# Attention in a two-layer decoder trunk: score products in two row halves, fp32 value products in two column halves a step later

## The chip, the core and the metric

The kernel runs on one core of one Trainium2 chip. The metric is the device time of one execution in microseconds (us); lower is better. TensorE is the matrix engine, VectorE and ScalarE do elementwise work, GpSimd (POOL) does elementwise work in SBUF, and SyncE (SP) issues the loads. The profile calls them PE (PEld for its weight loads), DVE, ACT, POOL and SP.

## The reference

The input x is 512 tokens by 1024 features, fp32. The model has two layers: an HGRN2 mixer with a conv FFN, then sliding-window attention with a conv FFN, and a final norm. What the change touches is the attention:

```python
def swa_sink_attention(x, k, v, w_q, sinks, w_o):
    q = (x @ w_q).reshape(b_, nb, WINDOW, ATT_KV_HEADS, ATT_GROUP, ATT_HEAD_DIM)
    ...
    scores = jnp.einsum('bnqkgd,bnskd->bnkgqs', q, kb) * ATT_HEAD_DIM ** -0.5
    scores = scores - slopes[:, :, None, None] * dist
    scores = jnp.where(valid[None, :, None, None], scores, -jnp.inf)
    m = jnp.maximum(jnp.max(scores, axis=-1, keepdims=True), sink)
    e = jnp.exp(scores - m)
    probs = e / (jnp.sum(e, axis=-1, keepdims=True) + jnp.exp(sink - m))
    out = jnp.einsum('bnkgqs,bnskd->bnqkgd', probs, vb)
    return out.reshape(b_, s_, ATT_Q_HEADS * ATT_HEAD_DIM) @ w_o
```

There are 16 query heads of 64 features and 2 key/value heads; head j uses key/value head 0 for j below 8 and 1 above. The window is 128, so each block of 128 queries sees its own 128 keys and the 128 before (the first block only its own).

## The kernel before, in words

Activations lie with features on the 128 partitions and the 512 tokens along the free dimension. Large products are done in the type fp32r with each operand split into a high and a low part: `three` (L110 to L113) issues high x high, high x low and low x high into one PSUM bank. `weights` (L94) loads a piece of 128x1024 by SP, copies it to its high part on ScalarE (L104) and subtracts for the low part on VectorE (L105). Plain fp32 products (the transposes, the norm's spread at L186, the HGRN2 products at L323 and L384) are issued without a split, and the profile shows each of the latter as two instructions.

The attention works in 8 steps j. A step handles heads j and j+8 together: the projection `queries(j)` gives one 128x512 bank with the 64 features of head j in the upper half of the partitions and those of head j+8 in the lower. It is a generator, so that its 24 products can be spread between other work: each `step(gen)` issues three of them, and the last also the evacuation (L670) and the split (L674, L675). Before the change the split writes, for each head, a tile whose own half is the high part of the query and whose other half is the low part; the keys' high and low parts stand in both halves (L642 to L645). So two products over all 128 contraction rows (L693) give all four partial products of a head: 8 products for the four blocks of queries. The values are split too, with zeros in the other head's columns (L630, L655, L656), so that all 24 value products of a step (L737) add into one bank `po` of 128 rows.

`softmax` (L696) adds the bias and takes the row maxima on VectorE (L701), exponentiates with a running sum on ScalarE (L708) and scales on POOL (L713). `turn` transposes the probabilities on TensorE (L721), copies them to a high part on ScalarE (L724) and subtracts for the low part on VectorE (L725).

`attend` writes out the order of a step: it interleaves the projection of step j+2, the scores and softmax of step j+1, and the transposes and value products of step j; the value bank is evacuated at its end (L771, L772). `early` fills the last two steps with products of the output projection. The order in which the code names instructions is their priority; a compiler pass orders each engine's queue by it and by readiness and inserts the semaphores. Tiles come from pools: `mm` and `bk` have two PSUM banks each, the score tiles `ax` two pairs of banks, weights three and raw weights four buffers.

Of the kernel before, what the change touches and what calls it, by code (L numbers as in the profile page):

```python
# [50 lines left out]
def trunk(ctx: ExitStack, tc: tile.TileContext, xT, vec, w_qf, w_ig, w_ho, w_kv, w_q, w_o,  # L51
# [19 lines left out]
    def slot(dt=F32):  # L71
        return act.tile([P, S], dt, tag="a", name=nm("a"))
# [4 lines left out]
    def mm_bank():  # L77
        return psm.tile([P, S], F32, tag="mm", name=nm("mm"))
# [16 lines left out]
    def weights(src, n, parts=1, beside=None):  # L95
        raw = wraw.tile([P, 1024], F32, tag="raw", name=nm("raw"))
        hi = wsp.tile([P, 1024], F32R, tag="whi", name=nm("whi"))
        lo = wsp.tile([P, 1024], F32R, tag="wlo", name=nm("wlo"))
        for i in range(parts):
            c = slice(i * n // parts, (i + 1) * n // parts)  # L100
            nc.sync.dma_start(raw[:, c], src[:, c])
            if beside:
                beside[0](i)
            A.copy(hi[:, c], raw[:, c])  # L104
            V.tensor_tensor(lo[:, c], raw[:, c], hi[:, c].bitcast(F32), op=ALU.subtract)  # L105
            if beside:
                beside[1](i)
        return hi, lo
# [27 lines left out]
    class Norm:  # L136
        def __init__(self, gains):
            self.gains = gains
            self.xs = [[None] * KT for _ in gains]
            self.acc = None  # L140
# [328 lines left out]
            flush()  # L469

    class Out:
        def __init__(self, w, piece, m0, banks):
            self.w, self.piece, self.m0, self.banks = w, piece, m0, banks

        def step(self, k, x):
            n = len(self.banks)
            kk = k % (KT // n)
            if kk == 0:
                self.hi, self.lo = weights(self.w[self.piece + k * n // KT], 1024)
            for i, ps in enumerate(self.banks):  # L480
                ws = slice((kk * n + i) * P, (kk * n + i + 1) * P)
                three(ps, self.hi[:, ws], self.lo[:, ws], *x, k == 0, k == KT - 1)
# [142 lines left out]


    halves = [slice(0, HD), slice(HD, P)]
    heads = lambda ap, g: ap.rearrange("p (t d) -> p t d", t=NT)[:, :, g * HD:(g + 1) * HD]
    k_hi, k_lo, v_hi, v_lo = ([slot(F32R) for _ in range(2)] for _ in range(4))
    for x in v_hi + v_lo:  # L630
        G.memset(x.bitcast(F32), 0.0)
    pk = any_bank()
    project(pk, w_kv[0], na.xs[0])
    na.stats()
# [1 line left out]
    project(pv, w_kv[1], na.xs[0], after={3: na.spread})  # L636
    kf = work("fr")
    V.tensor_tensor(kf, pk, na.bc, op=ALU.mult)
    for g in range(2):
        src = kf[halves[g]]  # L640
        own, other = halves[g], halves[1 - g]
        A.copy(k_hi[g][own], src)  # L642
        A.copy(k_hi[g][other], src)
        for dst in (own, other):
            V.tensor_tensor(k_lo[g][dst], src, k_hi[g][own].bitcast(F32), op=ALU.subtract)  # L645
    vf = work("fr")
    V.tensor_tensor(vf, pv, na.bc, op=ALU.mult)

    def token_values():
        pt = any_bank()  # L650
        for t in range(NT):
            ts = slice(t * P, (t + 1) * P)
            PE.transpose(pt[:, ts], vf[:, ts], ident)
        for g in range(2):
            A.copy(heads(v_hi[g], g), heads(pt, g))  # L655
            V.tensor_tensor(heads(v_lo[g], g), heads(pt, g), heads(v_hi[g], g).bitcast(F32),  # L656
                            op=ALU.subtract)

    spans = [(n, P if n == 0 else 2 * P) for n in range(NT)]

    def queries(j, qs):
        pq = mm_bank()
        hi, lo = weights(w_q[j], 1024)
        for k in range(KT):
            ks = slice(k * P, (k + 1) * P)
            three(pq, hi[:, ks], lo[:, ks], *na.xs[1][k], k == 0, k == KT - 1)
            if k < KT - 1:
                yield
        qf = work("qr")
        V.scalar_tensor_tensor(qf, pq, HD ** -0.5, na.bc, op0=ALU.mult, op1=ALU.mult)  # L670
        qs += [work("sg", dt=F32R), work("state", dt=F32R)]
        for g in range(2):
            own, other = halves[g], halves[1 - g]
            A.copy(qs[g][own], qf[own])  # L674
            V.tensor_tensor(qs[g][other], qf[own], qs[g][own].bitcast(F32), op=ALU.subtract)  # L675
        yield

    class Rows:
        def __init__(self, j, g, qs):
            self.hd, self.g, self.qs = j + 8 * g, g, qs  # L680
# [5 lines left out]
        def scores(self):  # L686
# [3 lines left out]
            for n, w in spans:  # L690
                keys = slice((n + 1) * P - w, (n + 1) * P)
                for i, k in enumerate((k_hi[self.g], k_lo[self.g])):
                    PE.matmul(self.sc[:, n, 0:w], self.qs[self.g][:, n * P:(n + 1) * P],  # L693
                              k[:, keys], start=i == 0, stop=i == 1)

        def softmax(self):  # L696
            mx, den, es = (small.tile([P, NT], F32, tag=t, name=nm(t))
# [17 lines left out]
        def turn(self, i):  # L715
            pt = bk_bank()
            width = (4 - i) * P
            for u in range(4 - i):
                n = 2 * i + (u + 1) // 2
                src = self.e[n // 2][:, n % 2, P:] if u % 2 == 0 else self.e[n // 2][:, n % 2, 0:P]  # L720
                PE.transpose(pt[:, u * P:(u + 1) * P], src, ident)  # L721
            eh = work("st" if i == 0 else "kst", dt=F32R)
            el = work("mva" if i == 0 else "fr", dt=F32R)
            A.copy(eh[:, 0:width], pt[:, 0:width])  # L724
            V.tensor_tensor(el[:, 0:width], pt[:, 0:width], eh[:, 0:width].bitcast(F32),  # L725
                            op=ALU.subtract)
            return eh, el

        def values(self, po, i, eh, el):
            vh, vl = v_hi[self.g], v_lo[self.g]  # L730
            for kb in range(2):
                b = 2 * i + kb
                w = P if b == NT - 1 else 2 * P
                src = slice(kb * 2 * P, kb * 2 * P + w)
                ws = slice(b * P, (b + 1) * P)
                for n3, (v, x) in enumerate(((vh, eh), (vh, el), (vl, eh))):
                    PE.matmul(po[:, b * P:b * P + w], v[:, ws], x[:, src],  # L737
                              start=self.g == 0 and b == 0 and n3 == 0,
                              stop=self.g == 1 and b == NT - 1 and n3 == 2,
                              skip_group_check=True)  # L740

    def step(gen, n=1):
        for _ in range(n):
            next(gen, None)

    def attend(rows, nxt, gen):
        a, b = rows
        step(gen, 2)
        for r in nxt[:1]:
            r.scores()  # L750
        po = mm_bank()
        step(gen)
        for r in nxt[:1]:
            r.softmax()
        a0 = a.turn(0)
        for r in nxt[1:]:
            r.scores()
        step(gen, 2)
        a1 = a.turn(1)
        b0 = b.turn(0)  # L760
        a.values(po, 0, *a0)
        for r in nxt[1:]:
            r.softmax()
        step(gen, 2)
        b1 = b.turn(1)
        step(gen)
        a.values(po, 1, *a1)
        b.values(po, 0, *b0)
        b.values(po, 1, *b1)
# [7 lines left out]
    rows = [Rows(0, g, qs[0]) for g in range(2)]  # L777
    step(queries(0, qs[0]), KT)
    gen = queries(1, qs[1])
    step(gen, 4)  # L780
    token_values()
    rows[0].scores()
    step(gen, 4)
    rows[1].scores()
    for r in rows:
        r.softmax()
    outs = []

    def early(j):
        if j == KT - 2:  # L790
            outs.append(Out(w_o, 6, 6, [mm_bank()]))
            for k in range(KT - 2):
                outs[0].step(k, mixed[k])
                yield
        else:
            outs.append(Out(w_o, 4, 4, aux_two()))
            for k in range(KT - 1):
                outs[1].step(k, mixed[k])
# [93 lines left out]
```

## Time and profile before

| | us |
|---|---|
| median of 3 runs | 1203.5 |
| lowest, highest | 1201.35, 1206.54 |
| the profiled execution | 1203.45 |
| its span | 1200.1 |
| PE busy | 1185.0 (99%) |
| DVE busy | 691.1 (58%) |
| ACT busy | 461.7 (38%) |
| POOL busy | 172.0 (14%) |

The span runs from the first to the last instruction that the profile records, and 3.35 us of the execution lie around it. Busy times of PE come from modelled ends of pipelined products, so two that follow each other overlap in the list; the difference of their starts is what one costs in a stream. A row of the timeline with xN is N instructions merged, with the time from the first start to the last end.

### The profile page before, as it was taken

What the parts mean: (1) busy time and instruction counts of PE and PEld (TensorE: products, weight loads), DVE (VectorE), ACT (ScalarE), POOL (GpSimd) and SP (SyncE); (2) the same over time, 40 slices, a digit from 0 to 9 for tenths busy, and PEclk for the clock granted to TensorE, in tenths of its full rate; (3) what the DMA queues carried; (4) which work ended last, traced back from release to release, by engine and by line L of the source; (5) the groups of instructions that cost most, each with busy time, mean ns of one, the idle gap of its engine ahead of it and who ended that gap; (6) DMA issues with size and microseconds to landing.
All of it is one profiled execution on the core that took longest, in us unless ns stands there. A gap on an engine that the chain in (4) does not pass through costs nothing.

```text
span 1200.1 us, 17055 instructions
## 1 busy us (share of the span) xinstructions
PE 1185.0 (99%) x6732; PEld 982.4 (82%) x6732; DVE 691.1 (58%) x1260; ACT 461.7 (38%) x858; POOL 172.0 (14%) x239
## 2 busy tenths in 40 slices
PE   9999999999999999999999999999999999999997
PEld 7888888878888888888888788887888888888887
DVE  6667676665555533555555688646555335555434
ACT  6444444443333222332244577634332222233223
POOL 0011111122111000110112244203111001011001
PEclk9999999999999999999999999999999999999999
DMA  7222222213222233322233211032322343232212
GB/s 244 89 73 80 78 72 71 72 53 106 88 105 77 73 97 123 98 95 84 73 97 121 69 51 43 30 95 84 102 88 66 88 132 101 88 100 94 88 53 71
DMA packets 35087, 105.36 MB, mean 88 GB/s; under 512 B 4032, under 2 KB 7232, under 8 KB 35008
## 3 DMA queue, kind: packets, MB, share of 16 engines
q1 hardware_dynamic: 33920, 103.24, 27.2%
q8 instruction: 52, 0.85, 0.3%
q10 hardware_dynamic: 1088, 1.05, 0.2%
q14 instruction: 27, 0.22, 0.1%
HBM read 102.18 MB, written 2.10 MB: 87 GB/s over the span
## 4 chain that ended last, share of the span: by engine, by line
PE 90%; DVE 3%; ACT 3%; issue 2%; POOL 1%; DMA 0%; SPq 0%; POOLq 0%; ACTq 0%; DVEq 0%
PE mm L111 13%; PE mm L112 13%; PE mm L113 13%; PE bk L111 11%; PE bk L113 11%; PE bk L112 11%; PE mm L252 7%; PE ax L113 2%; PE ax L111 2%; PE ax L112 2%; PE ax L323 1%; ACT ks L708 1%; DVE wlo L105 1%; ACT qp L708 1%; PE bk L411 1%
## 5 line engine op out<-in xcount | busy, mean ns | idle before, releaser
L104 ACT CAST whi<-raw 128x1024 fp32r<-128x1024 f32 (+3 forms) x208 | 199.1, 959 | 380.9 <-PE mm L112 175.7
L111 PE MATMUL mm<-a,whi 128*128 128x512 f32 x720 | 288.0, 400 | 0.0
L112 PE MATMUL mm<-a,whi 128*128 128x512 f32 x720 | 285.8, 397 | 0.0
L113 PE MATMUL mm<-a,wlo 128*128 128x512 f32 x720 | 285.6, 397 | 0.0
L105 DVE TENSOR_TENSOR wlo<-raw,whi 128x1024 fp32r<-128x1024 f32 (+3 forms) x208 | 234.5, 1128 | 65.5 <-ACT whi L104 65.3
L111 PE MATMUL bk<-a,whi 128*128 128x512 f32 x560 | 222.1, 397 | 0.0
L112 PE MATMUL bk<-a,whi 128*128 128x512 f32 x560 | 221.1, 395 | 0.3 <-DVE a L147 0.3
L113 PE MATMUL bk<-a,wlo 128*128 128x512 f32 x560 | 221.0, 395 | 0.0
L113 PEld LDWEIGHTS mm<-a,wlo 128*128 128x128 f32 x720 | 135.9, 189 | 30.7
L111 PEld LDWEIGHTS mm<-a,whi 128*128 128x128 f32 x720 | 136.0, 189 | 29.3 <-issue 0.2
L112 PEld LDWEIGHTS mm<-a,whi 128*128 128x128 f32 x720 | 136.0, 189 | 29.1 <-issue 0.2
L112 PEld LDWEIGHTS bk<-a,whi 128*128 128x128 f32 x560 | 105.5, 188 | 25.7 <-DVE a L147 0.7
L111 PEld LDWEIGHTS bk<-a,whi 128*128 128x128 f32 x560 | 105.5, 188 | 24.8 <-issue 0.5
L113 PEld LDWEIGHTS bk<-a,wlo 128*128 128x128 f32 x560 | 105.5, 188 | 24.6
L252 PE MATMUL mm<-whi,a 128*128 128x256 f32 x512 | 94.3, 284 | 0.7 <-ACT a L146 0.4
L252 PEld LDWEIGHTS mm<-whi,a 128*128 128x128 f32 x512 | 79.9, 190 | 2.4 <-ACT a L146 1.4
L513 ACT ACTIVATE qp<-qp 128x512 f32<-128x512 f32 x44 | 27.8, 632 | 128.2 <-DVE qp L512 128.2
L252 PE MATMUL mm<-wlo,a 128*128 128x256 f32 x256 | 72.5, 283 | 0.0
L514 POOL TENSOR_TENSOR qp<-qp,rbc 128x512 f32<-128x512 f32 x44 | 56.9, 1294 | 100.7 <-ACT qp L513 100.7
L506 POOL MEMSET ks<- 128x2 f32 x44 | 4.3, 100 | 447.1 <-DVE qp L512 435.1
L512 DVE SCALAR_TENSOR_TENSOR qp<-ks,vecs,qp 128x512 f32<-128x512 f32 x88 | 65.9, 749 | 1.7
L252 PEld LDWEIGHTS mm<-wlo,a 128*128 128x128 f32 x256 | 48.6, 190 | 0.3
(205 smaller groups left out, 1338.0 us busy)
## 6 DMA issues: line engine op xcount, KB each, us to landing
raw<-in_w_up_dram SPq DMA_DIRECT2D x88, 512.0 KB, 3.5
raw<-in_w_dn_dram SPq DMA_DIRECT2D x32, 320.0 KB, 2.8
raw<-in_w_qf_dram SPq DMA_DIRECT2D x16, 512.0 KB, 3.6
raw<-in_w_ig_dram SPq DMA_DIRECT2D x14, 512.0 KB, 3.5
raw<-in_w_dn_dram SPq DMA_DIRECT2D x16, 384.0 KB, 3.1
raw<-in_w_ho_dram SPq DMA_DIRECT2D x8, 512.0 KB, 3.5
raw<-in_w_q_dram SPq DMA_DIRECT2D x8, 512.0 KB, 3.4
raw<-in_w_o_dram SPq DMA_DIRECT2D x8, 512.0 KB, 3.5
```

The costliest lines, as they stand in the source:

```text
L104: A.copy(hi[:, c], raw[:, c])
L105: V.tensor_tensor(lo[:, c], raw[:, c], hi[:, c].bitcast(F32), op=ALU.subtract)
L111: PE.matmul(ps, ah, bh, start=first, stop=False)
L112: PE.matmul(ps, ah, bl, start=False, stop=False)
L113: PE.matmul(ps, al, bh, start=False, stop=last)
L252: PE.matmul(ps, x[:, ts], w[:, ws], start=k == 0 and t % 2 == 0 and i == 0, stop=k == KT - 1 and t % 2 == 1 and i == 2, skip_group_check=True)
L323: PE.matmul(ps[j * GRP:(j + 1) * GRP, c], ks[:, g * GRP:(g + 1) * GRP], mv[:, g], start=True, stop=True)
L411: PE.matmul(po[:, cols[c]], st[:, c], v[c], start=c == 0, stop=False, skip_group_check=True)
L512: V.scalar_tensor_tensor(c, gp[:, i:S + i], cw[i], c, op0=ALU.mult, op1=ALU.add)
L513: A.activation(c, c, AF.Silu)
L514: G.tensor_tensor(c, c, norm.bc, op=ALU.mult)
L708: A.activation(x, x, AF.Exp, bias=mx[:, n:n + 1], accum_out=den[:, n:n + 1])
```

## The change

Scores: the keys are kept once, split into high and low, with head j's in the upper and head j+8's in the lower 64 partitions. The query is split at full height. Each head's block then takes three products over its own 64 contraction rows (high x high, high x low, low x high), and the two heads' products alternate, in the upper and the lower half of the rows. Both heads' scores are written in one piece.

Values: neither the values nor the transposed probabilities are split. A head's block takes one fp32 product whose output is 64 rows: head j's in the upper and head j+8's in the lower half of the output partitions (the column halves of the array), alternating. They are put off: the transposes of step j are made in step j, its value products at the start of step j+1, right ahead of the scores of step j+2 (`close`, then `scores`).

Order: a step issues the last six of one query's eight groups of three products and, near its end, the first two groups of the next query's. The weights of a projection (and of the early output projection) are loaded by a call of their own ahead of its first product. Scores, `prepare` and `values` are functions of their own; the memsets of the values go.

```diff
@@ Out
-            if kk == 0:
-                self.hi, self.lo = weights(self.w[self.piece + k * n // KT], 1024)
+            self.load(k, n)
@@ keys and values
-    k_hi, k_lo, v_hi, v_lo = ([slot(F32R) for _ in range(2)] for _ in range(4))
-    for x in v_hi + v_lo:
-        G.memset(x.bitcast(F32), 0.0)
+    k_hi, k_lo = slot(F32R), slot(F32R)
+    vtok = slot()
...
+    A.copy(k_hi, kf)
+    V.tensor_tensor(k_lo, kf, k_hi.bitcast(F32), op=ALU.subtract)
...
+        A.copy(vtok, pt)
@@ queries
+        hi, lo = weights(w_q[j], 1024)
+        yield
         pq = mm_bank()
-        hi, lo = weights(w_q[j], 1024)
...
-        for g in range(2):
-            own, other = halves[g], halves[1 - g]
-            A.copy(qs[g][own], qf[own])
-            V.tensor_tensor(qs[g][other], qf[own], qs[g][own].bitcast(F32), op=ALU.subtract)
+        A.copy(qs[0], qf)
+        V.tensor_tensor(qs[1], qf, qs[0].bitcast(F32), op=ALU.subtract)
         yield
+    def scores(rows, qs):
+        for r in rows:
+            r.prepare()
+        for n, w in spans:
+            keys = slice((n + 1) * P - w, (n + 1) * P)
+            for i, (q, k) in enumerate(((0, k_hi), (0, k_lo), (1, k_hi))):
+                for r in rows:
+                    half = halves[r.g]
+                    PE.matmul(r.sc[:, n, 0:w], qs[q][half, n * P:(n + 1) * P], k[half, keys],
+                              start=i == 0, stop=i == 2)
+
+    def values(po, i, parts):
+        for kb in range(2):
+            b = 2 * i + kb
+            w = P if b == NT - 1 else 2 * P
+            src = slice(kb * 2 * P, kb * 2 * P + w)
+            for g in range(2):
+                PE.matmul(po[halves[g], b * P:b * P + w],
+                          vtok[:, b * P + g * HD:b * P + (g + 1) * HD], parts[g][:, src],
+                          start=b == 0, stop=b == NT - 1, skip_group_check=True)
@@ turn
-            eh = work("st" if i == 0 else "kst", dt=F32R)
-            el = work("mva" if i == 0 else "fr", dt=F32R)
-            A.copy(eh[:, 0:width], pt[:, 0:width])
-            V.tensor_tensor(el[:, 0:width], pt[:, 0:width], eh[:, 0:width].bitcast(F32),
-                            op=ALU.subtract)
-            return eh, el
+            et = work("st" if i == 0 else "kst")
+            A.copy(et[:, 0:width], pt[:, 0:width])
+            return et
@@ attend
+    def attend(rows, nxt, gen, after, ready):
         a, b = rows
         step(gen, 2)
         for r in nxt[:1]:
+            r.softmax()
+        first = [a.turn(0)]
         step(gen)
+        second = [a.turn(1)]
+        step(gen)
         for r in nxt[1:]:
             r.softmax()
+        first.append(b.turn(0))
         step(gen, 2)
+        ready()
+        step(after)
+        second.append(b.turn(1))
+        step(after)
+        return first, second
+
+    def close(first, second):
+        po = mm_bank()
+        values(po, 0, first)
+        values(po, 1, second)
         oh, ol = slot(F32R), slot(F32R)
         A.copy(oh, po)
@@ the loop
     for j in range(KT):
-        gen = queries(j + 2, qs[j + 2]) if j + 2 < KT else early(j)
-        nxt = [Rows(j + 1, g, qs[j + 1]) for g in range(2)] if j + 1 < KT else []
-        mixed.append(attend(rows, nxt, gen))
+        if j:
+            mixed.append(close(*turns))
+        nxt = [Rows(j + 1, g) for g in range(2)] if j + 1 < KT else []
+        if nxt:
+            scores(nxt, qs[j + 1])
+        gens.append(queries(j + 3, qs[j + 3]) if j + 3 < KT else early(j + 1))
+        turns = attend(rows, nxt, gens[j + 2], gens[j + 3], lambda: step(gens[j + 3]))
         rows = nxt
+    mixed.append(close(*turns))
```

## Rows read from the trace of the kernel before

**Rows 1.** The page: busy time of the engines, and the chain that ended last.
```profile
PE 1185.0 (99%) x6732; PEld 982.4 (82%) x6732; DVE 691.1 (58%) x1260; ACT 461.7 (38%) x858; POOL 172.0 (14%) x239
...
PE 90%; DVE 3%; ACT 3%; issue 2%; POOL 1%; DMA 0%; SPq 0%; POOLq 0%; ACTq 0%; DVEq 0%
```

**Rows 2.** Busy time by stretch: length, PE, PEld, DVE, ACT, POOL (instructions); clock; DMA share, GB/s.
```profile
677.26:699.90 22.64, 20.81 (x118) 17.35 (x116) 17.27 (x59) 16.98 (x50) 10.11 (x20) 0.92 0.16 47
...
712.53:724.64 12.11, 12.03 (x78) 10.49 (x78) 10.10 (x32) 8.90 (x26) 5.44 (x10) 1.00 0.13 45
```

**Rows 3.** TensorE in order of time, that step: start, duration, instruction, idle before.
```profile
712.53 1.21 PE L693 MATMUL ax<-a,sg 128*128 128x128 f32 x8 [0.63 <-DVE sg L675]
713.57 0.39 PE L111 MATMUL mm<-a,whi 128*128 128x512 f32 x1
...
714.27 0.49 PE L721 MATMUL bk<-cons,ks 128*128 128x128 f32 x3
...
717.72 0.36 PE L737 MATMUL mm<-st,a 128*128 128x256 f32 x1
...
718.50 0.39 PE L111 MATMUL mm<-a,whi 128*128 128x512 f32 x1
...
720.92 0.28 PE L737 MATMUL mm<-kst,a 128*128 128x256 f32 x1
...
722.86 0.27 PE L737 MATMUL mm<-kst,a 128*128 128x128 f32 x1
722.96 0.45 PE L111 MATMUL mm<-a,whi 128*128 128x512 f32 x1
```

**Rows 4.** TensorE in order of time, an fp32 product of 512 columns (L186).
```profile
665.25 1.02 PE L186 MATMUL ax<-kst,cons 128*128 128x512 f32 x2
...
666.34 0.39 PE L112 MATMUL bk<-a,whi 128*128 128x512 f32 x1
```

**Rows 5.** TensorE in order of time, fp32 products in column tiles; then their groups' means.
```profile
218.53 0.55 PE L323 MATMUL ax<-mvb,ks 128*32 128x48 f32 x32
...
221.98 0.40 PE L111 MATMUL mm<-a,whi 128*128 128x512 f32 x1
222.31 0.45 PE L384 MATMUL ax<-qp,ks 128*64 128x64 f32 x8
222.69 0.50 PE L112 MATMUL mm<-a,whi 128*128 128x512 f32 x1
...
L323 PE MATMUL ax<-mvb,ks 128*32 128x48 f32 x448 | 7.7, 209 | 0.7 <-DVE tot L347 0.7
...
L384 PE MATMUL ax<-qp,ks 128*64 128x64 f32 x56 | 3.2, 234 | 0.1
```

**Rows 6.** Groups of VectorE, 699.9 to 761 us: busy us, mean ns, idle before.
```profile
L725 DVE TENSOR_TENSOR mva<-bk,st 128x512 fp32r<-128x512 f32 x10 | 6.9, 690 | 1.6 <-ACT st L724 1.2
...
L725 DVE TENSOR_TENSOR fr<-bk,kst 128x384 fp32r<-128x384 f32 x10 | 5.5, 547 | 0.0
...
L675 DVE TENSOR_TENSOR sg<-qr,sg 64x512 fp32r<-64x512 f32 x5 | 4.3, 852 | 0.2
...
L675 DVE TENSOR_TENSOR state<-qr,state 64x512 fp32r<-64x512 f32 x5 | 3.8, 756 | 0.2
...
L670 DVE SCALAR_TENSOR_TENSOR qr<-mm,rbc 128x512 f32<-128x512 f32 x5 | 3.4, 680 | 0.0
```

**Rows 7.** Waits of TensorE and its weight loads, 699 to 790 us: total, times, longest.
```profile
PE ax L693 <- DVE sg L675: 1.1, 3, 0.6
...
PEld ax L693 <- DVE sg L675: 3.4, 5, 1.1
```

**Rows 8.** The loads of the query weights: issue ns, first and last start.
```profile
L101 SPq DMA_DIRECT2D raw<-in_w_q_dram x8: 327/328/328, 642.5 to 676.8; - x8
```

**Rows 9.** Busy time by stretch, around the first transposes (columns as rows 2).
```profile
686.00:690.00 4.00, 2.17 (x13) 1.49 (x12) 3.02 (x15) 3.03 (x11) 3.07 (x5) 0.98 0.16 16
...
690.10:693.10 3.00, 3.00 (x10) 2.40 (x9) 2.37 (x12) 2.54 (x11) 2.22 (x7) 0.50 0.40 150
```

More of the change, by code (lines that the diff above doesn't have):

```diff
@@ L471, in trunk, with __init__, load @@
     class Out:
-        def __init__(self, w, piece, m0, banks):
-            self.w, self.piece, self.m0, self.banks = w, piece, m0, banks
+        def __init__(self, w, piece, m0, banks=None):
+            self.w, self.piece, self.m0, self.banks, self.loaded = w, piece, m0, banks, -1
+        def load(self, k, n=1):
+            if self.loaded < k * n // KT:
+                self.loaded = k * n // KT
+                self.hi, self.lo = weights(self.w[self.piece + self.loaded], 1024)
         def step(self, k, x):
@@ L627, in trunk @@
     halves = [slice(0, HD), slice(HD, P)]
-    heads = lambda ap, g: ap.rearrange("p (t d) -> p t d", t=NT)[:, :, g * HD:(g + 1) * HD]
-    k_hi, k_lo, v_hi, v_lo = ([slot(F32R) for _ in range(2)] for _ in range(4))
-    for x in v_hi + v_lo:
-        G.memset(x.bitcast(F32), 0.0)
+    k_hi, k_lo = slot(F32R), slot(F32R)
+    vtok = slot()
     pk = any_bank()
@@ L638, in trunk @@
     V.tensor_tensor(kf, pk, na.bc, op=ALU.mult)
-    for g in range(2):
-        src = kf[halves[g]]
-        own, other = halves[g], halves[1 - g]
[L642 to L645, printed above, removed]
+    A.copy(k_hi, kf)
+    V.tensor_tensor(k_lo, kf, k_hi.bitcast(F32), op=ALU.subtract)
     vf = work("fr")
@@ L653, in token_values @@
             PE.transpose(pt[:, ts], vf[:, ts], ident)
-        for g in range(2):
-            A.copy(heads(v_hi[g], g), heads(pt, g))
-            V.tensor_tensor(heads(v_lo[g], g), heads(pt, g), heads(v_hi[g], g).bitcast(F32),
-                            op=ALU.subtract)
+        A.copy(vtok, pt)
     spans = [(n, P if n == 0 else 2 * P) for n in range(NT)]
     def queries(j, qs):
+        hi, lo = weights(w_q[j], 1024)
+        yield
         pq = mm_bank()
-        hi, lo = weights(w_q[j], 1024)
         for k in range(KT):
@@ L671, in queries, with __init__ @@
         qs += [work("sg", dt=F32R), work("state", dt=F32R)]
-        for g in range(2):
-            own, other = halves[g], halves[1 - g]
-            A.copy(qs[g][own], qf[own])
-            V.tensor_tensor(qs[g][other], qf[own], qs[g][own].bitcast(F32), op=ALU.subtract)
+        A.copy(qs[0], qf)
+        V.tensor_tensor(qs[1], qf, qs[0].bitcast(F32), op=ALU.subtract)
         yield
+    def scores(rows, qs):
[17 more added lines that the diff above has]
+                          start=b == 0, stop=b == NT - 1, skip_group_check=True)
     class Rows:
-        def __init__(self, j, g, qs):
-            self.hd, self.g, self.qs = j + 8 * g, g, qs
+        def __init__(self, j, g):
+            self.hd, self.g = j + 8 * g, g
             self.e = [work("ks", (P, 2, 2 * P), 4), work("qp", (P, 2, 2 * P), 4)]
@@ L684, in span, with prepare @@
             return self.e[n // 2][:, n % 2, 2 * P - w:]
-        def scores(self):
+        def prepare(self):
             self.bias = work("tot", (P, 2 * P), 4)
@@ L689, in scores @@
             self.sc = aux_pair()
[L690 to L694, printed above, removed]
         def softmax(self):
@@ L721, in turn @@
                 PE.transpose(pt[:, u * P:(u + 1) * P], src, ident)
-            eh = work("st" if i == 0 else "kst", dt=F32R)
-            el = work("mva" if i == 0 else "fr", dt=F32R)
-            A.copy(eh[:, 0:width], pt[:, 0:width])
-            V.tensor_tensor(el[:, 0:width], pt[:, 0:width], eh[:, 0:width].bitcast(F32),
-                            op=ALU.subtract)
-            return eh, el
[L729 to L740, printed above, removed]
+            et = work("st" if i == 0 else "kst")
+            A.copy(et[:, 0:width], pt[:, 0:width])
+            return et
     def step(gen, n=1):
@@ L744, in step @@
             next(gen, None)
-    def attend(rows, nxt, gen):
+    def attend(rows, nxt, gen, after, ready):
         a, b = rows
@@ L749, in attend @@
         for r in nxt[:1]:
-            r.scores()
-        po = mm_bank()
+            r.softmax()
+        first = [a.turn(0)]
         step(gen)
[L753 to L761, printed above, removed]
+        second = [a.turn(1)]
+        step(gen)
         for r in nxt[1:]:
             r.softmax()
+        first.append(b.turn(0))
         step(gen, 2)
[L765 to L769, printed above, removed]
+        ready()
[7 more added lines that the diff above has]
+        values(po, 1, second)
         oh, ol = slot(F32R), slot(F32R)
@@ L776, in trunk @@
     qs = [[] for _ in range(KT)]
[L777 to L780, printed above, removed]
-    token_values()
[L782 to L786, printed above, removed]
+    rows = [Rows(0, g) for g in range(2)]
+    step(queries(0, qs[0]), KT + 1)
+    gens = [None, queries(1, qs[1]), queries(2, qs[2])]
+    step(gens[1])
+    step(gens[1], 4)
+    token_values()
+    scores(rows, qs[0])
+    step(gens[2])
+    rows[0].softmax()
+    step(gens[1], 4)
+    rows[1].softmax()
+    step(gens[2], 2)
     outs = []
@@ L790, in early @@
         if j == KT - 2:
-            outs.append(Out(w_o, 6, 6, [mm_bank()]))
+            o = Out(w_o, 6, 6)
+            outs.append(o)
+            o.load(0)
+            yield
+            o.banks = [mm_bank()]
             for k in range(KT - 2):
-                outs[0].step(k, mixed[k])
+                o.step(k, mixed[k])
                 yield
-        else:
-            outs.append(Out(w_o, 4, 4, aux_two()))
+        elif j == KT - 1:
+            o = Out(w_o, 4, 4)
+            outs.append(o)
+            o.load(0, 2)
+            yield
+            o.banks = aux_two()
             for k in range(KT - 1):
-                outs[1].step(k, mixed[k])
+                o.step(k, mixed[k])
                 yield
     for j in range(KT):
-        gen = queries(j + 2, qs[j + 2]) if j + 2 < KT else early(j)
-        nxt = [Rows(j + 1, g, qs[j + 1]) for g in range(2)] if j + 1 < KT else []
-        mixed.append(attend(rows, nxt, gen))
+        if j:
[5 more added lines that the diff above has]
+        turns = attend(rows, nxt, gens[j + 2], gens[j + 3], lambda: step(gens[j + 3]))
         rows = nxt
+    mixed.append(close(*turns))
     nf = Norm([V_F1])
```

## The prediction

> **What bounds the kernel now.** I read the page first: TensorE is busy 99% of the span and the chain that ended last lies on it for 90% [rows 1]. So only time that leaves TensorE, or idle time on it, can change the end. Then the busy time by stretch. The change touches the attention, from about 677 to 785 us. One step of its loop, from the first score product to that of the next step, takes 12.11 us, with TensorE busy 12.03 at the full clock, VectorE 10.10 and ScalarE 8.90; the first stretch takes 22.64 us for what comes before the second step, at a granted clock of 0.92 [rows 2]. The other six steps of the loop last 12.0 to 12.6 us.
>
> Then one such step in order of time on TensorE [rows 3]. The durations printed there overlap, so I use start to start. Three query products take 713.57 to 714.27, or 0.233 each, and a step has 24: 5.6 us. The eight score products of one head take 712.53 to 713.57, 1.04 us, and there are two heads: 2.08. The value products take 717.72 to 718.50 for six and 720.92 to 722.96 for eighteen: 2.82. The rest, 1.6 us, is 14 transposes and a short wait. A product of 128 moving columns is no quicker than 0.10 to 0.12 (722.86 to 722.96), and 24 value products at an average of 0.1175 say that 256 columns cost about the same. I take 0.115 for one fp32r product of 128 or 256 columns.
>
> **Value products.** Removed: 24 fp32r products a step (2.82 us). Added: 8 fp32 products, four for each head, with 64 output rows, the heads' alternating between the two column halves. A head has 128+3x256 = 896 moving columns. The fp32 product of 512 columns at L186 shows two instructions and takes from 665.25 until the next product can stream, 666.34 less 0.23: 0.86 us [rows 4]. So 896 columns cost 0.86x896/512 = 1.50 us for a head, and 3.0 for both if they go one after the other. Do column halves run together? This kernel already has such products. At L384 eight instructions of 64 columns in column tiles span 0.45 with a mean of 0.234, so starts are (0.45-0.234)/7 = 0.031 apart, where 0.86/2x64/512 = 0.054 would be serial; at L323, four column tiles, (0.55-0.209)/31 = 0.011 against 0.040 [rows 5]. So halves overlap by 1.74 to 2: 1.50 to 1.72 us. Entering costs 222.31-221.98-0.23 = 0.10, leaving 222.69-222.31-8x0.031 = 0.13. I take 1.60+0.15 = 1.75, since the longer stream of 256 columns should lie nearer to full overlap than one of 64. Gain 1.07 a step, eight steps: **-8.6 us**.
>
> **Score products.** Removed: 16 a step (2.08). Added: 24, three for each head and block over 64 contraction rows, heads alternating between row halves and writing separate banks. No row shows two row halves at work. The bounds: together, twelve pairs of 0.115 = 1.38; one after the other, 24x0.115 = 2.76; 0.12 for entering on either. I take the lower end, because the nearest rows, the column tiles, overlap nearly fully in loading and in streaming [rows 5], and keep the upper as a rival. 1.50 against 2.08: -0.58, eight times: **-4.6 us**.
>
> **Transposes** keep their count, but stand in four groups a step instead of three, each with a switch between fp32 and fp32r of about 0.1 (the entering price): **+0.7 us**.
>
> **Work off TensorE.** The low half of the transposed weights goes (L725, 0.690 and 0.547, twice a step: 2.5 us of VectorE), and four half-height query copies and subtractions become two of full height, 0.852+0.756 down to about 0.69 on VectorE: 0.9 us [rows 6]. This is worth nothing directly, as TensorE ends last; it takes VectorE from 10.1 to about 6.7 and, if the copies shrink as the subtractions do, ScalarE from 8.9 to about 8.2 in a step that I expect to be 10.6 long. ScalarE is then four fifths full: the next to bound. The key and value preparation and the four memsets run beside the projections and cost nothing either way.
>
> **Waits that go.** The scores of a step wait for the query's low part (L675): 1.1 us in all as seen by the matmuls, 3.4 by the weight loads [rows 7]. The new order finishes that query a good 3 us of TensorE work earlier (six query products, three transposes, the value products). I take **-2.0 us**, between the two.
>
> **Waits that come.** (a) Where one query ends and the next begins there is nothing between them now: the first product of the next needs a bank of the pool of two while the old one waits for L670 (0.680) and its queue. The value bank is free by then, so the second bank should serve: 0, else about 0.9 for each of six such places. Behind a waiting TensorE stand the last transposes, and behind those the copy that the value products need. (b) The last transposes' copy has 0.7 us of products and the first half of the values, 0.85, as cover; it can queue behind an exponential on ScalarE. (c) The scores need the query split: three operations of 0.68 to 0.85 each plus queueing, against the 3 us named. Together 0 to 1.3 us a step, no gain possible; I take 0.3 over eight: **+2.4 us**. The weight loads that move issue no new transfers, and the w_q ones were all issued by 676.8 us, far ahead of use [rows 8], so SP's queue and the moved load cost nothing. POOL's bias and scaling keep their number.
>
> **The start.** Before the first turn TensorE is idle for some 1.8 of 4 us, and then runs 3 us at half clock, 0.50 [rows 9], which loses another 1.5. The new start has the same chain of softmax ahead of the first transposes and as little work to cover it. I take 0 and keep -3.5 and +2 for the range. After the last step the output projection of other heads covers the copies as before.
>
> **Sum:** -8.6-4.6+0.7-2.0+2.4 = -12.1. The profiled execution took 1203.45 us (span 1200.1), within 0.1 of the median 1203.5, so I forecast **1191.4 us**. All good bounds at once (values 1.65, scores 1.38, waits -3.4 and none new, start -3.5) would give 1182, all bad ones of the waits and the 1.72 of the values 1200; its own range is 1184 to 1198.
>
> **Rivals.** *The row halves do not overlap.* Each of the 24 products brings its own 128 weight columns, and if loads go one after the other the price is 2.88 a step instead of 1.50: +1.38x8 = +11, **1202.5**, no change. For it: a product of 128 columns takes as long as one of 256, so a weight load sets the pace [rows 3]. Against: loads in different column tiles plainly overlap: 32 instructions, each with its own load, in 0.55 us [rows 5]. The Trainium skill bears on this rival (TensorE: Matmul & The Clock Gate, "LDWEIGHTS (loading the stationary operand)"): a load's time goes by the columns, not by contraction rows, so that 64 rows save nothing; by an estimate from its formula, 128/1.2 = 107 ns, 24 loads would be 2.56 us, which is more than the removed 2.08. The same page's part on packing small matmuls says that loads overlap where the row group differs, which would give the lower end; no row here decides between them.
>
> *The bank is not there.* The wait (a) comes true: six times 0.9 to 1.5, +5.4 to +9: **1197 to 1200**, with a wait of a query product for L670 in the profile.
>
> *Slower: one gap a step that also drops the clock.* With values and scores in one piece, both of their inputs are needed at one place. If TensorE stands idle there as long as at the start, 1.8 us, and pays the half clock afterwards, 1.5, that is 3.3 for each of seven steps, +23: **1214**. It decides from about (12.1+6)/7 = 2.6 us a step upward. For it: ScalarE's load and the chain through it; against: the half clock was seen after one gap only, and the waits of 0.6 at the step's head have left the clock at 1.00 [rows 2, 3].
>
> *The column halves go one after the other* with four cycles a column: +1.3x8, **1201 to 1204**, and slower only with the row halves failing too. Rows 5 speak against it.
>
> **Numbers.** Chances: forecast 0.60, row halves 0.14, bank 0.12, gap 0.09, column halves 0.05. A measurement of this kernel tells about 0.5% (6 us) from no change, so faster means under 1197.5. Nearly all of the first case and a third of the bank's lie there, with a little of the row case if the start gains too: 0.65. Most of the row and column cases and the rest of the bank's are the same: 0.22. Slower, 0.13, is the gap, and row halves that fail together with the bank or the column halves. The range that leaves out no more than 2 in 10: 1183 to 1204.
>
> **What would show it.** Right: value products of one step within 1.9 us, scores within 1.7, a step of about 10.6, the wait of scores for L675 gone, clock 1.00 in the steps. Wrong: score starts 0.11 apart throughout, idle time of query products released by L670, of value products by ScalarE's copy, or a granted clock under 1 after the step's head.

## The result, and the profile after

The changed kernel takes 1189.38 us (median of 4 runs, 1188.89 to 1190.72), the kernel before 1202.42 beside it; the ratio is 0.9893, with an interval of 0.9878 to 0.9908. The forecast was 1191.4. The profiled execution has a span of 1187.1 against 1200.1, so its 13.0 us are those of the medians, and the trace can stand for the runs. Lines of the changed kernel: scores L679, values L688, transposes L730 with their copy at L732, the query's evacuation and split at L665, L667 and L668, row maxima L710 and L713, exponentials L717.

The page of the changed kernel, as [rows 1]:

```profile
PE 1175.2 (99%) x6732; PEld 967.3 (81%) x6732; DVE 663.4 (56%) x1215; ACT 452.8 (38%) x846; POOL 173.0 (15%) x235
...
PE 96%; ACT 1%; issue 1%; DVE 1%; POOL 1%; DMA 0%; POOLq 0%; SPq 0%; ACTq 0%
```

TensorE still ends last, and more purely: the chain lies on it for 96% instead of 90%. Its busy time fell by 9.8 us, the span by 13.0; the other 3.2 were idle time. VectorE lost 27.7 us of work, which the forecast counted as worth nothing in itself.

Busy time by stretch, columns as [rows 2]: the second step to begin, a full step, and the first 12 us of softmax and transposes in three slices:

```profile
685.56:695.94 10.38, 10.38 (x76) 7.69 (x75) 6.68 (x28) 8.71 (x27) 7.13 (x14) 1.00 0.16 51
...
717.30:728.39 11.09, 11.07 (x79) 8.67 (x78) 7.22 (x26) 7.96 (x26) 5.76 (x11) 1.00 0.17 49
...
684.00:688.00 4.00, 4.00 (x40) 3.29 (x39) 2.12 (x5) 2.91 (x10) 3.61 (x6) 1.00 0.02 6
688.00:692.00 4.00, 4.00 (x23) 3.29 (x22) 3.55 (x20) 3.50 (x13) 2.09 (x5) 1.00 0.41 131
692.00:696.00 4.00, 4.00 (x26) 2.15 (x24) 1.56 (x6) 3.87 (x12) 3.05 (x7) 1.00 0.00 0
```

A step from scores to scores takes 10.4 to 11.1 us where it took 12.1 to 12.6. In the last three lines TensorE has neither the idle time nor the granted clock of 0.50 that [rows 9] show before the first transposes and after them. The whole attention, from the transposes of the values to the end of the last value product, takes 676.97 to 771.54, 94.6 us, against 677.26 to 785.00, 107.7: **-13.2**. The rest of the kernel is unchanged, and its time agrees within 0.2. The first product behind the attention in the kernel before:

```profile
785.00 0.45 PE L111 MATMUL mm<-a,whi 128*128 128x512 f32 x1
```

TensorE in order of time (start, duration, instruction): an early value block, then a full step, then the last value block:

```profile
703.81 0.65 PE L688 MATMUL mm<-st,a 128*64 128x256 f32 x2
704.38 0.50 PE L111 MATMUL mm<-a,whi 128*128 128x512 f32 x1
...
705.05 0.86 PE L688 MATMUL mm<-st,a 128*64 128x256 f32 x5
...
706.70 0.33 PE L679 MATMUL ax<-a,sg 64*128 64x128 f32 x2
...
721.52 0.49 PE L730 MATMUL bk<-cons,qp 128*128 128x128 f32 x3
...
722.54 0.40 PE L111 MATMUL mm<-a,whi 128*128 128x512 f32 x1
...
723.48 0.40 PE L112 MATMUL mm<-a,whi 128*128 128x512 f32 x1
723.89 0.52 PE L730 MATMUL bk<-cons,ks 128*128 128x128 f32 x3
...
726.41 1.16 PE L688 MATMUL mm<-st,a 128*64 128x256 f32 x7
...
727.54 0.92 PE L688 MATMUL mm<-kst,a 128*64 128x256 f32 x7
728.39 0.44 PE L679 MATMUL ax<-a,sg 64*128 64x128 f32 x4
...
729.54 0.40 PE L679 MATMUL ax<-a,sg 64*128 64x256 f32 x4
...
729.99 0.50 PE L111 MATMUL mm<-a,whi 128*128 128x512 f32 x1
...
769.88 1.08 PE L688 MATMUL mm<-st,a 128*64 128x256 f32 x8
770.80 0.82 PE L688 MATMUL mm<-kst,a 128*64 128x256 f32 x8
771.54 0.50 PE L111 MATMUL mm<-a,whi 128*128 128x512 f32 x1
```

Read start to start. **Scores:** 728.39 to 729.99, 1.60 us for 24 products. **Values:** the last block has nothing in its way and takes 769.88 to 771.54, 1.66; the one of the full step takes 726.41 to 728.39, 1.98; the early one is cut in two by two query products, 0.57 for its first two instructions and 1.65 for the rest, 2.22. The eight blocks are 2.22, 2.22, 2.16, 1.98, 1.98, 1.95, 1.92 and 1.66, together 16.1, against 8 x 2.82 = 22.6. **Transposes:** before the third group stands 0.41 (723.48 to 723.89) where a query product costs 0.23, a wait of 0.18; two of the eight steps have one. A group without a wait costs no more than its products: three transposes and the three query products behind them take 721.52 to 722.54, 1.02, which is 3 x 0.109 and 3 x 0.233.

ScalarE in the same step (idle before it in brackets):

```profile
721.11 0.30 ACT L714 ACTIVATE es<-mx,vecs 128x4 f32<-128x4 f32 x1 [3.12 <-DVE mx L713]
...
726.08 0.57 ACT L732 COPY st<-bk 128x512 f32<-128x512 f32 x1
726.55 0.62 ACT L667 CAST sg<-qr 128x512 fp32r<-128x512 f32 x1
727.07 0.48 ACT L732 COPY kst<-bk 128x384 f32<-128x384 f32 x1
```

It idles 3.1 us until the row maxima come, then works without a gap: exponentials first, then the copies of the second head's transposes. The value block begins at 726.41, while the copy of that head's first half (`st`) still runs, 726.08 to 726.65. In an undisturbed block the products of the two heads start in pairs, both at 692.33 for example. Here one stream starts at 726.41 and the other, by the start of each product in the trace, at 726.70, 0.05 us after the end of that copy. The other blocks between 715 and 760 us show the same: the second stream starts at 715.61, 737.80, 748.65 and 759.51, each 0.05 after the end of its `st` copy. That is the new wait. It is not for the last copy (`kst`, 727.07 to 727.55), since the loss is there before: seven `st` products take 726.41 to 727.32, as long as eight do in the last block (769.88 to 770.80). TensorE shows no idle time for it, because one head's products run meanwhile, with the other column half empty; in the early blocks other products are drawn ahead as well.

### The profile page after: what moved, and what is told of

Its sections match the earlier page's. It is cut to its first block, busy times and chain, and to the rows that moved or that the text cites. A ratio compares the mean times of both kernels' runs of the same rounds, so it can differ in the third digit from the quotient of the medians.

```text
span 1187.1 us, 16984 instructions
## 1 busy us (share of the span) xinstructions
PE 1175.2 (99%) x6732; PEld 967.3 (81%) x6732; DVE 663.4 (56%) x1215; ACT 452.8 (38%) x846; POOL 173.0 (15%) x235
## 4 chain that ended last, share of the span: by engine, by line
PE 96%; ACT 1%; issue 1%; DVE 1%; POOL 1%; DMA 0%; POOLq 0%; SPq 0%; ACTq 0%
PE mm L111 14%; PE mm L112 14%; PE mm L113 14%; PE bk L111 11%; PE bk L113 11%; PE bk L112 11%; PE mm L252 8%; PE ax L111 2%; PE ax L113 2%; PE ax L112 2%; PE mm L688 1%; PE ax L679 1%; PE bk L730 1%; PE ax L323 1%; PE bk L411 1%
```

## The experiments

Each changes the changed kernel (ratio 0.9893) unless it says otherwise; times are told as ratios to the kernel before, 0.001 being 1.2 us. The changed kernel itself, timed a second time, gave 0.9906 (below), so differences between runs not made side by side are good to about 2 us.

**Scores, one head after the other.** The loop over heads moves outside:

```diff
-        for n, w in spans:
...
-            for i, (q, k) in enumerate(((0, k_hi), (0, k_lo), (1, k_hi))):
-                for r in rows:
...
+        for r in rows:
...
+            for n, w in spans:
...
+                for i, (q, k) in enumerate(((0, k_hi), (0, k_lo), (1, k_hi))):
```

> The changed kernel with the score products of one head issued all twelve in a row, then the other head's: same products, same banks, no alternation between the row halves. If the row halves overlap, a step's block of 24 grows from 1.60 us to about 2.9 (24 x 0.115 + 0.12), eight blocks: +10 us, about 1199. Rival, that 64-row products are simply cheap one by one (cheaper load): the block stays at 1.6 us and the time at 1189.

Measured: 0.9967 (0.9955 to 0.998), about +8.9 us. TensorE in one block:

```profile
721.23 0.43 PE L679 MATMUL ax<-a,sg 64*128 64x128 f32 x2
...
722.49 0.51 PE L679 MATMUL ax<-a,sg 64*128 64x128 f32 x4
...
722.88 0.45 PE L679 MATMUL ax<-a,sg 64*128 64x256 f32 x2
...
723.29 0.40 PE L679 MATMUL ax<-a,sg 64*128 64x256 f32 x2
...
724.09 0.50 PE L111 MATMUL mm<-a,whi 128*128 128x512 f32 x1
```

The same 24 products take 2.86 us instead of 1.60. One place inside tells it best: where the last block of one head meets the first of the other, the queue alternates them, and six products take 722.49 to 722.88, 0.39 us; the next three, of one head alone, take 0.41. Two row halves at work cost as much as one. That is +1.26 x 8 = +10; the value block before it is back at 1.74 (its copy has more time), which gives some back.

**Values, one head after the other.** `close` calls the values of one head, then of the other:

```diff
...
-        values(po, 0, first)
-        values(po, 1, second)
+        for g in range(2):
+            values(po, 0, first, g)
+            values(po, 1, second, g)
```

> The changed kernel with one head's four fp32 value products in a row, then the other's: no alternation between the column halves. If the column halves overlap, a block of 16 instructions grows from 1.66 to 1.98 us to about 3.0 (2 x 1.50), eight blocks: +8 to +10, about 1198. Rival, that fp32 products of 64 output rows cost half of the 128-row price by themselves: block unchanged, 1189.

Measured: 0.9946 (0.9934 to 0.9959), about +6.4 us. TensorE in one block:

```profile
727.63 1.08 PE L687 MATMUL mm<-st,a 128*64 128x256 f32 x4
728.54 0.38 PE L687 MATMUL mm<-kst,a 128*64 128x256 f32 x1
728.55 0.43 PE L687 MATMUL mm<-st,a 128*64 128x256 f32 x1
...
729.47 0.81 PE L687 MATMUL mm<-kst,a 128*64 128x256 f32 x4
730.21 0.44 PE L679 MATMUL ax<-a,sg 64*128 64x128 f32 x4
```

The block takes 2.58. The expected size was too high because the queue still mixed the heads in the middle. The three parts say it: four instructions of one head 0.91, eight of both heads 0.93 (728.54 to 729.47), four of the other head 0.74. Two column halves cost as much as one, for fp32 too.

**The values in three split products again**, in the new order: split values, split transposed weights, 24 products over full height:

```diff
...
-            et = work("st" if i == 0 else "kst")
-            A.copy(et[:, 0:width], pt[:, 0:width])
-            return et
+            eh = work("st" if i == 0 else "kst", dt=F32R)
+            el = work("mva" if i == 0 else "fr", dt=F32R)
+            A.copy(eh[:, 0:width], pt[:, 0:width])
+            V.tensor_tensor(el[:, 0:width], pt[:, 0:width], eh[:, 0:width].bitcast(F32),
+                            op=ALU.subtract)
+            return eh, el
```

> The changed kernel with the value products as before the change (values and transposed probabilities split, 24 fp32r products over 128 rows a step), in the new order. TensorE alone: 2.82 for 1.98 us a step, +0.85 x 8 = +7, 1196. Rival, that the saved VectorE work (2.5 us a step) is what counts, since the copies and subtractions stand ahead of the value products: waits at the step's head come on top, 1200 or more.

Measured: 0.9978 (0.9969 to 0.9987), +10.2 us. Of that, 24 products at the 2.82 of before against eight blocks of 16.1 in all are 8 x 2.82 - 16.1 = +6.5. The rest shows on TensorE, at the end of a value block:

```profile
720.09 0.40 PE L112 MATMUL mm<-a,whi 128*128 128x512 f32 x1
720.42 0.33 PE L685 MATMUL ax<-a,sg 64*128 64x128 f32 x1
720.78 0.39 PE L698 MATMUL mm<-kst,a 128*128 128x256 f32 x1
721.10 0.43 PE L685 MATMUL ax<-a,sg 64*128 64x128 f32 x3
```

Other products are drawn in between the value products, and with each change between half and full height a single product costs 0.32 to 0.36 instead of 0.12. A low part that is made after the copy is what they would be filling for; that is read, not tried, so the rival, waits that come with VectorE's work, stands for this part. The new order with the old value products thus keeps only 2.6 us of the gain (0.9978).

**The scores at full height again**: keys in both halves, half-height query splits, 16 products:

```diff
...
-                    PE.matmul(r.sc[:, n, 0:w], qs[q][half, n * P:(n + 1) * P], k[half, keys],
-                              start=i == 0, stop=i == 2)
+                    PE.matmul(r.sc[:, n, 0:w], qs[r.g][:, n * P:(n + 1) * P],
+                              k[:, keys], start=i == 0, stop=i == 1)
```

> The changed kernel with the score products as before the change (16 products over 128 rows, query and keys split into half-height tiles), in the new order. TensorE alone: 2.08 for 1.60 us a step, +0.5 x 8 = +4, 1193. Rival, that the four half-height split operations in place of two delay the scores: waits of the scores for the query's low part return, +0.3 to 0.6 a step more, 1196 to 1198.

Measured: 0.9955 (0.9941 to 0.9968), about +7.4 us, the rival's size. TensorE:

```profile
718.98 0.22 PE L685 MATMUL ax<-a,sg 128*128 128x128 f32 x1
...
719.92 1.09 PE L685 MATMUL ax<-a,sg 128*128 128x128 f32 x7
...
721.78 0.40 PE L111 MATMUL mm<-a,whi 128*128 128x512 f32 x1
...
728.29 0.65 PE L694 MATMUL mm<-st,a 128*64 128x256 f32 x2
728.87 0.51 PE L111 MATMUL mm<-a,whi 128*128 128x512 f32 x1
...
730.55 0.50 PE L113 MATMUL mm<-a,wlo 128*128 128x512 f32 x1
...
731.28 0.86 PE L694 MATMUL mm<-kst,a 128*64 128x256 f32 x6
```

Fifteen score products take 1.86 (719.92 to 721.78), and one stands alone ahead of them, 0.15 (718.98): 2.0 together. In the changed kernel it is 1.60 and another 0.10, by which the query product behind them is longer (718.90 to 719.23). That is +2.4 over eight. The larger part lies elsewhere: the value block now falls into three pieces with query and score products between; with these counted at 0.233 and 0.12 it takes some 2.7 us against 1.98. The four half-height query operations stand in the queues of the engines that owe the copies and the scores' inputs. This part is read from the trace; it was not tried by itself.

**The kernel before with one softmax named earlier**, the only change of order that could be made there alone:

```diff
     rows[0].scores()
+    rows[0].softmax()
     step(gen, 4)
     rows[1].scores()
-    for r in rows:
-        r.softmax()
+    rows[1].softmax()
```

> The kernel before with one line moved: at the start of the attention the first head's softmax is issued ahead of the second query's last four groups of products and its split, as in the changed kernel. If that order is what took the idle time and the half clock out of the start, about 3 us go: 1199 to 1200, with the granted clock at 1.00 in the stretch to 700 us. Rival, that the narrower split or the score block did it: no change, 1202 to 1203.

Measured: 1.0003 (0.9994 to 1.0012). Its profile has the granted clock at 1.00 through the start, but TensorE still waits there for POOL's scaling, 0.39 us here and 0.55 at 686.34:

```profile
685.45 0.33 PE L721 MATMUL bk<-cons,ks 128*128 128x128 f32 x1 [0.39 <-POOL ks L713]
```

Its attention is 1.7 us shorter in the profile and its median is not: named order alone buys nothing that can be measured.

**The changed kernel with the first softmax named later:**

```diff
-    rows[0].softmax()
     step(gens[1], 4)
+    rows[0].softmax()
     rows[1].softmax()
```

> The changed kernel with both softmaxes of the start issued behind the second query's products and split, as before the change. If the order matters: idle time ahead of the first transposes and a half clock come back, +3, 1192. Rival: the shorter split (two operations for four) covers it, no change, 1189.

Measured: 0.9907 (0.9894 to 0.9921), about +1.7 us, within the scatter. TensorE waits once and the clock stays at 1.00, so the half clock did not come back:

```profile
694.75 0.32 PE L679 MATMUL ax<-a,sg 64*128 64x128 f32 x1 [0.28 <-ACT sg L667]
```

**The copy for the second half of the values on VectorE:**

```diff
-            A.copy(et[:, 0:width], pt[:, 0:width])
+            if i == 0:
+                A.copy(et[:, 0:width], pt[:, 0:width])
+            else:
+                V.tensor_copy(et[:, 0:width], pt[:, 0:width])
```

> The changed kernel with the copy of the second half of the transposed probabilities (128x384) on VectorE in place of ScalarE. The last value block of the attention, with no softmax beside it, takes 1.66 us, the others 1.92 to 2.2. If the others wait for that copy behind exponentials on ScalarE, they come down to about 1.7: -0.3 x 7 = -2 us, 1187. Rival, that the block's length is TensorE's own: no change, 1189; VectorE has 3.5 us to spare in a step, so no loss is expected.

Measured: 0.988 (0.9865 to 0.9895), 1187.31 us, -1.6 as expected. TensorE in one step:

```profile
725.93 1.19 PE L688 MATMUL mm<-st,a 128*64 128x256 f32 x8
726.84 0.92 PE L688 MATMUL mm<-kst,a 128*64 128x256 f32 x8
727.69 0.44 PE L679 MATMUL ax<-a,sg 64*128 64x128 f32 x4
```

The moved copy runs at once (725.34 to 725.90 on VectorE). The block does not wait for it, but with both moved copies gone from ScalarE's row the `st` copy, for which it does wait, ends at 725.98, 0.05 behind the start of the block instead of 0.24 (726.65 against 726.41). So 1.98 has become 1.76, and 1.67 in the later steps; the eight blocks take 14.6 together instead of 16.1, which is the gain. Both kernels once more, on one chip:

> The changed kernel itself, timed on one chip beside the version with the copy on VectorE, so that the two share the runs of the kernel before. Theory (ScalarE's queue ahead of the last copy costs about 0.2 us a step, and the attention's 94.6 us are that much too long): ratio about 0.9893, that is 1.5 to 2 us above the other. Rival (the difference of the two seen so far was the scatter of runs on different chips): the two within 0.5 us.

> The last copies on VectorE, beside the changed kernel on one chip. Theory: ratio about 0.988, 1.5 to 2 us below the changed kernel, attention 92.8 us against 94.6 in the trace. Rival: the two medians within 0.5 us, although the trace's attention is shorter.

Measured: the changed kernel 1190.24 us, 0.9906 (0.9888 to 0.9924), attention 677.00 to 771.64; the copy on VectorE 1188.59 us, 0.9888 (0.9872 to 0.9905), attention 676.91 to 769.67. So 94.6 and 92.8 in the traces, spans 1186.9 and 1184.8, medians 1.65 apart. The intervals overlap, but two pairs of runs and two pairs of traces say the same 1.6 to 2 us. In both pairs this version is the faster.

**With that copy, the last transposes one group of products earlier:**

```diff
-        step(after)
         second.append(b.turn(1))
+        step(after)
         step(after)
```

> On top of the copy on VectorE: the last transposes of a step stand ahead of both groups of the next query's products instead of between them, so that their copy has 1.4 us of products as cover instead of 0.7. Theory (what is left of the value block's excess over 1.66 us is the wait for that copy): the value blocks of the later steps come down from 1.67-1.76 to about 1.66, the waits of the kst products for the copy (6 of them, 2.1 us in the loads' rows) go, 1 to 2 us in all: about 1186. Rival (the compiler fills the wait already, and what is left is the price of the pieces into which the value block falls in the first steps): within 0.5 us of the copy on VectorE alone, 1187.

Measured: 0.9892 (0.9875 to 0.991), 1188.34 us: no gain, the rival's size but not its reason, that the compiler fills the wait. The steps between scores are 10.19, 10.65 and 10.58 us, and 10.19, 10.64 and 10.57 without the move. The move took place: the last copy now ends at 726.25, well before a block that begins at 726.72. But its second stream starts at 726.81, behind the `st` copy on ScalarE (726.18 to 726.75), and the block takes 1.74. So the last copy was not what the block waited for.

**With that copy, the second head's transposes named together:**

```diff
         first.append(b.turn(0))
+        second.append(b.turn(1))
         step(gen, 2)
         ready()
         step(after)
-        second.append(b.turn(1))
         step(after)
```

> On top of the copy on VectorE: all transposes of the second head stand in one group, as before the change, so that a step has three groups of transposes and not four. Theory (each group pays an entry and an exit between fp32 and fp32r products, about 0.2 us together): the transposes of a step go from 1.76 to about 1.5 us, 1 to 2 us in all, and the copy of the last ones has two query steps and two of the next one's as cover: 1185 to 1186. Rival (the pool of two banks for transposes makes the second group wait for the copy of the group before it, some 0.5 us on ScalarE): no gain or up to 3 us worse, 1187 to 1190.

Measured: 0.9881 (0.9865 to 0.9898), 1187.57 us, the same as with the copy alone. It was no clean test of the number of groups: the compiler kept two query products between the two, so there are still four. But TensorE shows an early value block that no longer falls apart:

```profile
703.15 1.08 PE L688 MATMUL mm<-st,a 128*64 128x256 f32 x8
...
704.82 0.50 PE L111 MATMUL mm<-a,whi 128*128 128x512 f32 x1
```

1.67 us, the price of the last block of the changed kernel, and four groups of transposes cost 1.54 in a step without a wait (the one that begins at 737.62), as in the changed kernel (739.49). The attention is 92.2 us long. What is left on TensorE in a step of 10.6 us is 24 query products at 0.233, 1.60, 1.67 and 1.5, which is 10.4: products and the changes between their forms, and hardly a wait.

## Why the prediction was right

The sum came out at -12.1 and the time at -13.0. The terms, by the profile (the attention's -13.2), with the changes into and out of a block counted as the forecast counted them:

| term | forecast | profile |
|---|---|---|
| value products without waits | -8.6 | 8 x (1.66+0.10-2.82) = -8.5 |
| waits that come | +2.4 | 16.1-8 x 1.66 = +2.8 |
| score products | -4.6 | 8 x (1.60+0.10-2.08) = -3.0 |
| transposes | +0.7 | about +2.0 |
| start | 0 | -1.8-1.5 = -3.3 |
| waits that go | -2.0 | 2.2 down to 0.2 = -2.0 |

Together these are -12.0. Of the other 1.2, some 0.9 is that the eight value blocks before took 23.5 in all, and not 8 x 2.82. The mechanisms came in the main as written. That the sum is within 1 us is in part luck: the three rows of products were forecast at -12.5 and are -9.5, and the start, put at nothing, makes up for it.

**Values: right.** The block was put at 1.75 with its entry. It is 1.66 undisturbed and 0.10 for entering (the query product at 726.08 is followed 0.33 later, not 0.23); the 0.86 us of the norm's spread [rows 4] and the overlap of the column tiles [rows 5] carried over to streams four times as long. The run with one head after the other shows the overlap.

**Waits that come: the right size, and nearly the right reason.** Of the three, (a) did not happen: no query product waits for its bank (L665). (c) was one wait of 0.4 us. (b) came in kind: a copy that stands behind exponentials on ScalarE holds the value products. But the forecast named the last copy, and it was the one before it, of the second head's first half; only the first block of all waits for the last copy (it ends at 694.92, and the products cut off start at 695.15). The wait measures 0.26 to 0.32 in the four steps from 726 us on, 0.50 in the third block and 0.56 in the first two. The rows of weight loads, by what they waited for:

```profile
PEld mm L688 <- DVE den L718: 1.4, 4, 0.4
...
PEld ax L679 <- ACT sg L667: 0.4, 1, 0.4
```

The 1.4 put down to L718 is no wait. The value products do not read that tile, and the weight loads show the same 0.36 of idle time ahead of the block at 692.33, whose two streams start together.

**Scores: right in mechanism; this is the term that was sized worst.** What was added: the four blocks of queries take 0.39, 0.41, 0.35 and 0.45, the last with the change back to full height (729.54 to 729.99), and the query product behind 0.10 more: 1.70 and not 1.50, though a pair within a stream costs 0.12, as taken. What was removed: the 2.08 held more than score products. Before, eight of them behind a group of transposes take 1.02 and behind query products 0.93 (699.90 to 700.83), so that the end of a group of transposes was counted in them:

```profile
714.62 1.18 PE L693 MATMUL ax<-a,state 128*128 128x128 f32 x8
715.64 0.40 PE L111 MATMUL mm<-a,whi 128*128 128x512 f32 x1
```

The rival that row halves do not overlap fell by the run with one head after the other, which took 2.86 for what the rival put at 2.88. The Trainium skill (TensorE: Matmul & The Clock Gate, "Part 3: Packing small matmuls — row/col tiling") says that a weight load overlaps with products in flight only where the row group differs; the 0.39 for six products of both halves against 0.41 for three of one agrees.

**Transposes: mis-sized.** They were costed at one more change of form, 0.1 a step. The rows show no such price: 14 x 0.109 is 1.53, and four groups without a wait take 1.54. Read start to start they were 1.36 before only because the end of two groups was counted in the score and value products behind, as just shown, so the rows of values, scores and transposes are best read together. In two steps the wait of 0.18 makes it 1.76.

**Start: kept out of the sum, and its good bound came true.** The forecast took 0 and kept -3.5 for the range; the profile gives back the idle 1.8 and the half clock 1.5 of [rows 9]. With both heads' scores in one piece the first exponentials begin at 681.3 instead of 683.7 and the first transposes run without a wait. How much of it stands in the medians is open: the kernel before with an earlier softmax has the full clock too in its profile, and no better median. The link to scores in one piece was not tried by itself, so the cause of this part stays open.

**The other rivals.** No gap fell on the head of a step, and the clock stayed at 1.00 in all of them, so the slower case had no ground. ScalarE, named as the next to bound, is busy 8.0 of 11.1 us, but its work is not spread: it idles for the maxima and then runs in one go, and by the trace that, not its load, set the wait.

## What to carry to other kernels

Two products that use half the array each are worth interleaving instruction by instruction: here, in halves of the rows, six cost what three cost, and in halves of the columns eight what four cost. Where products are put off so that they stand in one piece, look for the operations that feed them in the queue of their engine, and shorten that queue. To find which of them is late, compare the start of each product with the ends of the copies: the cost shows as a longer block, not as idle time. A start price from a neighbouring kernel line (a column tile of 64, a spread of 512) was good to 5% when it was read start to start.

## What was not expected of the hardware

A change between half and full height or width costs TensorE time, and a change of type alone did not here. A single product between others of another height takes 0.32 to 0.36 us, where one in a stream takes 0.12, and entering a block of column halves costs 0.10; but transposes in fp32 and query products in fp32r, both at full size, follow each other for the sum of their prices (1.02 for three and three). The Trainium skill (TensorEngine Tiling (Array Packing), "Key Properties") says that a change of tiling mode drains the engine; these rows agree and give it a price.

A late input can leave no idle time on TensorE at all. With two column halves, the head that is ready runs alone and the block grows from 1.66 to about 1.95; in the early steps other products are drawn ahead, and the block becomes 2.2 in pieces.
